# A two-layer Hyena and attention trunk on one core: attention listed ahead of Hyena, filter weights four weight blocks sooner, owed vector work capped after an opening, one skip addition fewer

## The chip, the cores and the metric

The kernel runs on one core of a Trainium2 chip. The metric is the device time of one execution in microseconds; runs are compared by their median.

## The reference

The input is one sequence of 256 positions with 1024 channels, in fp32. Two layers follow each other; each is a SwiGLU block (hidden width 2688), a mixer, and a second SwiGLU block, all with RMSNorm ahead and a residual behind. The mixer runs two branches on the same input and adds them through sigmoid gates:

```python
for l in range(DEPTH):
    x = x + 0.5 * swiglu(rms_norm(x, ffn1_norm[l]), ...)
    x = x + hybrid_mixer(rms_norm(x, mix_norm[l]), ...)
    x = x + 0.5 * swiglu(rms_norm(x, ffn2_norm[l]), ...)
# hybrid_mixer, branch A (Hyena): z, x1, x2 = short_conv3(h @ w_in[hyena])
kf = hyena_filters(...)          # sin(sin(z @ w1 + b1) @ w2 + b2) @ w3, decayed, normalised, rfft
for o, gate in enumerate((x1, x2)):
    z = gate * (long_conv(z, kf[:, o]) + hy_skip[o] * z)
# branch B (attention): q, k RMS-normed per head; 12 heads in 3 dilation groups; softmax over 193 strided keys
y = (sigmoid(gA) * (y_hy @ w_hy_proj) + sigmoid(gB) * (y_at @ w_at_proj)) @ w_out
```

## The kernel before

**Weights and slots.** Every product is fp32 accuracy made of three fp32r products (high times high, high times low, low times high). So each weight block of 128x1024 floats is loaded by the sync queue into one of four `raw` buffers, copied to its high half `whi` by the scalar engine (ACT, line 151), and subtracted to its low half `wlo` by the vector engine (DVE, line 58, the helper through which most vector work goes, so all of it carries that line). Seven `whi`/`wlo` pairs are in flight. TensorE (PE) uses one block in one *slot*, mostly 24 matmuls of 128x256 on line 89. I number the blocks of layer 0 as w0, w1, ... in the order of loading: w0 to w64 are the first SwiGLU block (`ffn(l, 1)`), w65 to w68 the first q/k block and w69 to w80 the Hyena columns of the mixer's projection, w81 to w94 the other q, k and v blocks, w95 to w110 the gates, w111 on the merges. Layer 1 repeats this.

**Order of the work.** The program is emitted under `manual_schedule`, so each engine runs its instructions in the order in which Python emits them. `slot()` first calls `tick(room)`, which advances generators ("side chains") that hold everything that isn't a weight block, then emits the matmuls. `retire` emits the `whi` and `wlo` of later blocks and the evacuation of the finished accumulator. `tick` goes through the list `side` in its order, and stops when `owed`, an estimate of the vector work emitted and not yet done, reaches `room`; `passed` takes 2.43 from it per slot. A chain that has just yielded True isn't taken up again until its own work is estimated done (`due`). `drain(ended, room)` advances the side chains without any slot between them until a condition holds.

**Side chains.** In `ffn(l, 1)` the chain is `filters(l)` (in layer 0 also `tables`): a product with `fc`, a sine (vector arithmetic on `sd`, then the scalar engine's Sin, line 578), a second such pair, `st`, then for each of two orders a slot `fw3_unit` with the third filter weight (where the constant `FW3` says: after the evacuation of row block m = 10 and m = 20, so at w22 and w43), the decay product `k`, squares `sq` whose sum is transposed on PE (`s<-ident,sq`), a power on GpSimd (POOL), `rb`, `nb`, and the Fourier products `s<-hl,dft` into `spec`. In the mixer the chains are `hyena()`, `attention()` and one `qknorm(blk)` per q/k block, which squares (`sq`, ACT), sums (`ss`, DVE), takes a power on POOL (`rs<-ss,mhalf`, line 877), multiplies (`qk<-qk,rs`, DVE) and transposes on PE (`x<-ident,qk`). `conv(pr)` evacuates a Hyena pair with taps on DVE (`c<-acc,cw,c`) and transposes it (`x<-ident,c`, line 750). One step of `attention()` is: transposes of the last scores (`x<-ident,at`), values (`x<-v,at`), and new scores (`x<-qkT,...`), which DVE biases and ACT exponentiates (line 934). `gate(m)` starts with a drain until `spec0` (m below 4) or `spec1` (m from 4 on) is in `ready`, which Hyena adds when it has read that part of `spec`; gate 4 begins at w103. After the last gate a drain runs all side chains to their ends, then the merges use Hyena's output `u` (high and low half) and attention's `yaT`.

**PSUM.** Accumulators `acc` rotate over 3 banks, `x` over 3, `s` over 2. In `ffn(l, 1)` row block m uses the same `acc` bank as m + 3, so the matmuls of m + 3 wait until the two vector instructions of m's evacuation (`t<-t,acc`) have read it.

Of the kernel before, what the change touches and what calls it, by code (L numbers as in the profile page):

```python
# [37 lines left out]
ROOM = (0.9, 2.2, 2.5, 1.5, 1.5)  # L38
OVER = 0.07
MARGIN = 0.2  # L40
UNIT = 2.43
DEFER = 4
LEAD = 1
FW3 = (10, 20)


@with_exitstack
def hybrid_trunk(ctx: ExitStack, tc: tile.TileContext, a: dict, out: bass.AP):
# [4 lines left out]
    owed = [0.0]  # L53
# [154 lines left out]
    def await_(g):  # L208
        due[g] = min(owed[0], 2 * UNIT)

    def tick(room):
        for g in list(urgent):
            if due.get(g, 0.0) <= MARGIN and step(g) == "end":
                urgent.remove(g)
        live = [g for g in side if due.get(g, 0.0) <= MARGIN]
        while live and owed[0] < room:
# [14 lines left out]
    def flush():  # L231
        if pend:
            done, evac = pend.pop()
            retire(evac, done)

    def slot(fn, w, done=1, evac=None, room=0.0):
        if pend and getattr(pend[0][1], "first", False):
            flush()
        if room:
            tick(room)  # L240
        flush()
        while ptr["lo"] <= w:
            pump_lo()
        fn(*pairs[w])
        passed(UNIT)
        pend.append((done, evac))
# [104 lines left out]
    def opening(acc, evac, n):  # L351

        us = [use() for _ in range(4)]
        per = n // P

        def part(i, j):
            g, k = divmod(i, per)
            return xstat({j: acc[j][g]}, k, n, (j,), g * n if acc[j][0] is acc[j][-1] else 0, j == 0 and i > 1)

        for i in range(4):  # L360
            while ptr["lo"] <= us[i]:
                pump(1)
            part(i, 0)(*pairs[us[i]])
            if i in FEAT1:
                features(1, i - FEAT1[0])()
            for _ in range(FILL[i]):
                pump(1)
        evac(0)
        for i in range(4):
            u = us[i]  # L370
            slot(part(u - us[0], 1), u, evac=(lambda: evac(1)) if i == 3 else None)


    def proj_out(nk, lhs, coef, gain, tags=("x", "acc", "acc", "acc")):
# [172 lines left out]
    def filters(l):  # L547
        def gen(fp):
# [47 lines left out]
            for o in range(2):  # L596
# [52 lines left out]
                for i in range(2):  # L649
                    for j in range(2):  # L650
                        t = sd[j, i]
                        TT(out=t, in0=t, in1=nb, op=ALU.mult)
                        if j == 0:
                            TT(out=t[0:1, :], in0=t[0:1, :], in1=sk[:, o, :], op=ALU.add)
                        yield False
                for i in range(2):
# [68 lines left out]
    def mixer(l, gain):  # L725
        with tc.tile_pool(name=nm("mix"), bufs=1, reuse_waits="tile") as mp:
# [265 lines left out]
            for blk in range(5):  # L992
                n = 512 if blk < 4 else 256
                acc = [bank("acc") for _ in range(2)]
                last = n // 128 - 1
                if blk == 0:
                    opening([[b] for b in acc], qkv_out(blk, n, acc), n)
                    gens = [hyena(), attention()]
                    side.extend(gens)
                    for pr in range(6):  # L1000
                        pb = bank("acc")
                        slot(wstat(pb, sls[0]), use(), room=ROOM[0])
                        slot(wstat(pb, sls[1]), use(), evac=conv(pr)(pb), room=ROOM[0])
                else:
                    out_j = qkv_out(blk, n, acc)

                    def both(f=out_j):
                        f(0)
                        f(1)

                    both.first = True
                    for i in range(last + 1):
                        slot(xstat(acc, i, n), use(), evac=both if i == last else None,
                             room=ROOM[1])
# [217 lines left out]
```

## Time and profile before

| | before |
|---|---|
| runs | 1118.97, 1120.11, 1120.43 us; median 1120.11 |
| profiled execution | 1119.33 us, span 1117.5 us |
| granted TensorE clock, mean | 0.999 |
| PE busy | 1102.4 us, 99% of the span |
| DVE, ACT, POOL busy | 840.2, 643.3, 64.4 us |
| chain that ended last | PE 82%, DVE 8%, DMA 5%, ACT 3% |

The profiled execution's time has 1.8 us outside the span. A share is of the span; a row of a timeline gives start, duration, engine, line, operation, output and inputs by the program's names, and in brackets the idle time just before it with what ended it.

### The profile page before, as it was taken

To read this page: it belongs to the slowest core of one execution; us is meant where nothing else is said; L and a number is where in the kernel's file an instruction comes from. 1 tells how busy PE (TensorE), PEld (TensorE's weight loads), DVE (VectorE), ACT (ScalarE), POOL (GpSimd) and SP (SyncE) were. 2 spreads that over 40 slices of the span, in tenths; PEclk is the share of its full clock that TensorE was granted. 3 is DMA by queue.
4 is the path that set the end of the run, shared out by engine and by line. 5 is a ranking of instruction groups with operands and counts; after the bars stand their busy time and mean duration, and the time that the engine had idled before them with its cause. 6 is when DMAs were issued, how large, how long until landed. Compare 5 with 4: busy or idle time off the path is not lost.

```text
span 1117.5 us, 19195 instructions
## 1 busy us (share of the span) xinstructions
PE 1102.4 (99%) x7591; PEld 1029.3 (92%) x7591; DVE 840.2 (75%) x1243; ACT 643.3 (58%) x983; POOL 64.4 (6%) x113
## 2 busy tenths in 40 slices
PE   9999999999999999999999999999999999999998
PEld 8999988998999999998899998889989998999997
DVE  6779896788865877777567789868888667777772
ACT  6566754665655556666456665547565554666651
POOL 5100000011200000000000000001012000000000
PEclk9999999999999999999999999999999999999999
DMA  8756666556433746667746665737465245666671
GB/s 302 234 168 210 201 212 184 170 171 189 150 115 108 234 140 201 195 193 235 252 147 201 192 209 174 244 110 240 156 185 156 86 125 205 200 192 193 189 256 64
DMA packets 58845, 206.35 MB, mean 185 GB/s; under 512 B 7058, under 2 KB 7718, under 8 KB 58756
## 3 DMA queue, kind: packets, MB, share of 16 engines
q1 hardware_dynamic: 57764, 203.10, 57.3%
q0 software_dynamic: 704, 1.97, 0.6%
q8 instruction: 59, 0.97, 0.4%
q14 instruction: 30, 0.25, 0.1%
q10 hardware_dynamic: 288, 0.07, 0.0%
HBM read 204.00 MB, written 1.11 MB: 184 GB/s over the span
## 4 chain that ended last, share of the span: by engine, by line
PE 82%; DVE 8%; DMA 5%; ACT 3%; issue 2%; POOL 0%; SPq 0%; ACTq 0%; DVEq 0%; POOLq 0%
PE acc L89 54%; PE x L89 13%; PE s L89 12%; DMA raw<-in_gu 4%; DVE wlo L58 3%; PE x L102 2%; DVE spec L58 1%; ACT whi L151 1%; DVE t L58 1%; DVE xn L58 1%; ACT sq L285 1%; DVE x L58 1%; DVE hT L58 1%; PE x L750 1%; PE s L102 0%
## 5 line engine op out<-in xcount | busy, mean ns | idle before, releaser
L58 DVE TENSOR_TENSOR wlo<-raw,whi 128x1024 fp32r<-128x1024 f32 (+1 forms) x380 | 457.6, 1210 | 54.8 <-ACT whi L151 54.5
L151 ACT ACTIVATE whi<-raw 128x1024 fp32r<-128x1024 f32 (+1 forms) x380 | 392.8, 1046 | 142.3 <-PE acc L89 52.6
L89 PE MATMUL acc<-hT,whi 128*128 128x256 f32 (+1 forms) x2416 | 463.5, 290 | 0.0
L89 PEld LDWEIGHTS acc<-hT,whi 128*128 128x128 f32 x2416 | 379.6, 192 | 8.2 <-issue 1.3
L89 PE MATMUL acc<-hT,wlo 128*128 128x256 f32 x1360 | 367.1, 275 | 0.0
L89 PEld LDWEIGHTS acc<-hT,wlo 128*128 128x128 f32 x1360 | 260.9, 192 | 1.9
L89 PE MATMUL acc<-whi,hid 128*128 128x512 f32 (+1 forms) x378 | 115.5, 357 | 0.0
L89 PE MATMUL acc<-whi,hT 128*128 128x256 f32 (+1 forms) x576 | 115.2, 328 | 0.0
L89 PE MATMUL x<-whi,hid 128*128 128x512 f32 x336 | 112.1, 380 | 0.0
L89 PE MATMUL s<-hT,whi 128*128 128x512 f32 x304 | 104.0, 383 | 0.0
L89 PEld LDWEIGHTS acc<-whi,hT 128*128 128x128 f32 x576 | 88.0, 191 | 8.6 <-ACT hT L317 1.1
L89 PEld LDWEIGHTS acc<-whi,hid 128*128 128x128 f32 x378 | 71.0, 189 | 8.6
L89 PE MATMUL s<-hT,wlo 128*128 128x256 f32 x304 | 76.7, 273 | 0.0
L89 PEld LDWEIGHTS x<-whi,hid 128*128 128x128 f32 x336 | 63.6, 189 | 7.9
L89 PE MATMUL acc<-wlo,hid 128*128 128x512 f32 (+1 forms) x189 | 66.4, 356 | 0.0
L89 PEld LDWEIGHTS s<-hT,whi 128*128 128x128 f32 x304 | 57.7, 190 | 6.9 <-DVE c L58 0.7
L89 PE MATMUL acc<-wlo,hT 128*128 128x256 f32 (+1 forms) x288 | 63.4, 324 | 0.4 <-DVE wlo L58 0.2
L89 PE MATMUL x<-wlo,hid 128*128 128x512 f32 x168 | 63.7, 379 | 0.0
L481 ACT ACTIVATE hid<-t 128x256 fp32r<-128x256 f32 x38 | 19.9, 523 | 70.1 <-DVE t L58 70.1
L89 PEld LDWEIGHTS s<-hT,wlo 128*128 128x128 f32 x304 | 58.1, 191 | 1.9
L58 DVE TENSOR_TENSOR hid<-t,hid 128x256 fp32r<-128x256 f32 x76 | 35.5, 466 | 22.4 <-ACT hid L481 22.4
L58 DVE SCALAR_TENSOR_TENSOR t<-t,acc 128x256 f32<-128x256 f32 x46 | 19.2, 417 | 43.0 <-ACT t L457 33.1
(189 smaller groups left out, 1297.4 us busy)
## 6 DMA issues: line engine op xcount, KB each, us to landing
raw<-in_gu SPq DMA_DIRECT2D x152, 512.0 KB, 4.3
raw<-in_dn SPq DMA_DIRECT2D x84, 512.0 KB, 4.4
raw<-in_win_q SPq DMA_DIRECT2D x32, 512.0 KB, 4.0
raw<-in_wg SPq DMA_DIRECT2D x32, 512.0 KB, 4.2
raw<-in_win_h SPq DMA_DIRECT2D x24, 512.0 KB, 4.5
raw<-in_gx SPq DMA_DIRECT2D x16, 512.0 KB, 5.0
raw<-in_wo SPq DMA_DIRECT2D x16, 512.0 KB, 4.1
raw<-in_wp SPq DMA_DIRECT2D x16, 384.0 KB, 3.0
```

What stands on the lines that cost most here:

```text
L58: return f(**kw)
L89: nc.tensor.matmul(o, l, r, start=start, stop=stop)
L102: nc.tensor.transpose(b[:, q * P:(q + 1) * P], ap, ident)
L151: act(out=pairs[v][0][:, :n], in_=raws[v][:, :n], func=AF.Copy)
L285: act(out=sq, in_=x[:, j, sl], func=AF.Square, scale=1.0 / 32.0, accum_out=nst[j][:, h:h + 1])
L481: act(out=hi, in_=tv, func=AF.Copy)
L750: nc.tensor.transpose(tb[j][:, (q0 + i) * P:(q0 + i + 1) * P], c[:, i, 1 + j:1 + S:2], ident)
```

## The change

Four edits. `opening()` (the first four blocks of a stage) ends by lowering `owed` to at most 2.0, so that side chains may go on sooner. `FW3` moves the first third-filter-weight slot from after m = 10 to after m = 8 (w22 to w18; the second stays at w43). The skip term is added only for i = 0, in place of i = 0 and 1: one vector addition of one row (1x512) fewer per order and layer, four in all; no reader sees another value, since the odd part's first row has a factor of zero. In the mixer `attention()` stands ahead of `hyena()` in the list of side chains.

```diff
--- before.py
+++ after.py
@@ -38,10 +38,11 @@
 ROOM = (0.9, 2.2, 2.5, 1.5, 1.5)
 OVER = 0.07
 MARGIN = 0.2
+OPEN = 2.0
 UNIT = 2.43
 DEFER = 4
 LEAD = 1
-FW3 = (10, 20)
+FW3 = (8, 20)
 
 
 @with_exitstack
@@ -369,6 +370,7 @@
         for i in range(4):
             u = us[i]
             slot(part(u - us[0], 1), u, evac=(lambda: evac(1)) if i == 3 else None)
+        owed[0] = min(owed[0], OPEN)
 
 
     def proj_out(nk, lhs, coef, gain, tags=("x", "acc", "acc", "acc")):
@@ -650,7 +652,7 @@
                     for j in range(2):
                         t = sd[j, i]
                         TT(out=t, in0=t, in1=nb, op=ALU.mult)
-                        if j == 0:
+                        if j == 0 and i == 0:
                             TT(out=t[0:1, :], in0=t[0:1, :], in1=sk[:, o, :], op=ALU.add)
                         yield False
                 for i in range(2):
@@ -995,7 +997,7 @@
                 last = n // 128 - 1
                 if blk == 0:
                     opening([[b] for b in acc], qkv_out(blk, n, acc), n)
-                    gens = [hyena(), attention()]
+                    gens = [attention(), hyena()]
                     side.extend(gens)
                     for pr in range(6):
                         pb = bank("acc")
```

No instruction is added. What moves is the order. Three places follow; the change's own lines are one higher (L59 for L58), and numbers behind a name tell buffers apart.

First place: DVE, first SwiGLU block of layer 0. `t` and `hid` belong to evacuations, `sd` to the sines. Before, from the evacuation of m = 3 (`acc_529`) to that of m = 4 (`acc_596`):

```order
L58 SCALAR_TENSOR_TENSOR t_607<-t_607,acc_529 128x256
L58 TENSOR_TENSOR t_607<-t_607,acc_529 128x256
L58 TENSOR_TENSOR wlo_567<-raw_473,whi_566 128x1024
L58 TENSOR_TENSOR hid_212<-t_607,hid_193 128x256
L58 TENSOR_TENSOR wlo_605<-raw_503,whi_604 128x1024
L58 SCALAR_TENSOR_TENSOR t_674<-t_674,acc_596 128x256
L58 TENSOR_TENSOR t_674<-t_674,acc_596 128x256
```

Now, from the block behind the evacuation of m = 3 to the evacuation of m = 4 (`acc_608`):

```order
L59 TENSOR_TENSOR wlo_579<-raw_473,whi_578 128x1024
L59 TENSOR_TENSOR hid_212<-t_619,hid_193 128x256
L59 TENSOR_TENSOR wlo_617<-raw_507,whi_616 128x1024
L59 TENSOR_SCALAR sd_238<-s_683,fc_231 128x256
L59 TENSOR_SCALAR sd_238<-sd_238 128x256 x2
L59 SCALAR_TENSOR_TENSOR sd_238<-sd_238 128x256 x3
L59 TENSOR_SCALAR sd_238<-sd_238 128x256
L59 SCALAR_TENSOR_TENSOR t_696<-t_696,acc_608 128x256
L59 TENSOR_TENSOR t_696<-t_696,acc_608 128x256
```

The whole second sine has moved in ahead of the evacuation of m = 4; the first sine stands with its first half ahead of the evacuation of m = 2 and with its second half ahead of that of m = 3. Before, both sines came behind m = 4.

Second place: DVE, start of the mixer. `ss` are the sums of the q/k norm, `rs` is POOL's power, `c` the Hyena taps. Before:

```order
L58 TENSOR_REDUCE ss_2662<-sq_2664 128x8
L58 TENSOR_TENSOR wlo_2667<-raw_2568,whi_2666 128x1024
L58 TENSOR_REDUCE ss_2662<-sq_2709 128x8
L58 TENSOR_SCALAR ss_2662<-ss_2662 128x16
L58 TENSOR_TENSOR wlo_2712<-raw_2601,whi_2711 128x1024
L58 SCALAR_TENSOR_TENSOR c_2426<-acc_2661,cw,c_2426 128x256 x4
L58 TENSOR_TENSOR u_2423<-x_2702,u_2422 128x512
L58 TENSOR_TENSOR u_2423<-x_2703,u_2422 128x512
L58 TENSOR_TENSOR wlo_2746<-raw_2635,whi_2745 128x1024
L58 TENSOR_TENSOR qk_2435<-qk_2435,rs_2663 128x512
```

Now:

```order
L59 SCALAR_TENSOR_TENSOR c_2424<-acc_2530,cw,c_2424 128x256 x4
L59 TENSOR_REDUCE ss_2562<-sq_2598 128x8
L59 TENSOR_SCALAR ss_2562<-ss_2562 128x16
L59 TENSOR_TENSOR wlo_2601<-raw_2522,whi_2600 128x1024
L59 TENSOR_TENSOR qk_2433<-qk_2433,rs_2563 128x512
L59 TENSOR_TENSOR wlo_2640<-raw_2536,whi_2639 128x1024
L59 SCALAR_TENSOR_TENSOR c_2425<-acc_2596,cw,c_2425 128x256 x4
L59 TENSOR_TENSOR qk_2433<-qk_2433,rs_2563 128x512
```

From the second sum to the product with `rs` there were seven rows between, now there are two; the first taps stand ahead of the second sum in both. On PE the transposes of `qk` came behind w78 and w80 and now come behind w73 and w74, those of the first `c` behind w73 and now behind w72.

Third place: PE, ahead of w103 (gate 4). `odd` is the room that holds the scores of head 2. Before, from the end of w102 to the first matmuls of w103:

```order
L102 MATMUL x_3749<-ident,at_3593 128x128 x4
L89 MATMUL x_3756<-v_2432,at_3593 128x64 x4
L89 MATMUL x_3763<-qkT_3269,qkT_2820 128x128 x2
L89 MATMUL x_3763<-qkT_3460,qkT_2820 128x128
L89 MATMUL x_3763<-qkT_3460,qkT_3269 128x128
L89 MATMUL acc_3782<-hT,whi_3513 128x256 x2
L89 MATMUL acc_3782<-hT,wlo_3514 128x256
```

Now:

```order
L103 MATMUL x_3748<-ident,at_3626 128x128 x4
L90 MATMUL x_3755<-v_2430,at_3626 128x64 x4
L90 MATMUL x_3762<-qkT_3274,qkT_2676 128x128 x2
L90 MATMUL x_3762<-qkT_3469,qkT_2676 128x128
L90 MATMUL x_3762<-qkT_3469,qkT_3274 128x128
L103 MATMUL x_3781<-ident,odd_3619 128x128 x4
L90 MATMUL x_3787<-v_2430,at_3626 128x64 x4
L90 MATMUL x_3794<-qkT_3274,odd_3618 128x128 x2
L90 MATMUL x_3794<-qkT_3469,odd_3618 128x128
L90 MATMUL x_3794<-qkT_3469,odd_3619 128x128
L90 MATMUL acc_3780<-hT,whi_3513 128x256 x2
```

Two steps of attention now follow each other in the drain with no slot between them, so `x<-ident,odd`, which reads the second row group's scores, comes right behind them; before, w103 lay between. Behind w110, before the merges, attention's last two values and its last transposes stood (`x<-ident,at`, `x<-v,at` twice, `x<-ident,ya`); now only Hyena's last transposes `s<-ident,tt` stand there, with the copy and subtraction into `u`, and attention has ended at w109.

## Rows read from the trace of the kernel before

**Rows 1.** The page: busy time, share of the span, instructions of each engine.

```profile
PE 1102.4 (99%) x7591; PEld 1029.3 (92%) x7591; DVE 840.2 (75%) x1243; ACT 643.3 (58%) x983; POOL 64.4 (6%) x113
```

**Rows 2.** Waits of PE, whole span: total us, times, longest.

```profile
PE s L89 <- DVE hl L58: 2.3, 2, 1.4
PE s L102 <- DVE sq L58: 1.5, 1, 1.5
PE x L89 <- DVE st L58: 1.2, 1, 1.2
```

**Rows 3.** Timeline, layer 0, start of the mixer: start, duration, engine, line.

```profile
219.80 1.66 DVE L58 SCALAR_TENSOR_TENSOR c<-acc,cw,c 128x256 f32<-128x256 f32 x4 [1.56 <-ACT c L770]
224.12 0.66 PE L750 MATMUL x<-ident,c 128*128 128x128 f32 x4
224.53 0.47 PE L89 MATMUL acc<-hT,whi 128*128 128x256 f32 x2
227.43 0.68 DVE L58 TENSOR_REDUCE ss<-sq 128x8 f32<-128x512 f32 x1
228.25 1.23 DVE L58 TENSOR_TENSOR wlo<-raw,whi 128x1024 fp32r<-128x1024 f32 x1
228.40 3.84 POOL L877 TENSOR_TENSOR rs<-ss,mhalf 128x16 f32<-128x16 f32 x1 [26.33 <-DVE ss L58]
```

**Rows 4.** The tile rs and its readers, whole span: ns min/median/max.

```profile
L58 DVE TENSOR_TENSOR qk<-qk,rs x12: 678/685/693, 233.8 to 848.5; 128x512 f32<-128x512 f32 x12
L877 POOL TENSOR_TENSOR rs<-ss,mhalf x6: 2898/3842/3850, 228.4 to 842.0; 128x16 f32<-128x16 f32 x6
```

**Rows 5.** Timeline, layer 0, an attention step: PE, DVE, ACT.

```profile
318.70 0.47 PE L89 MATMUL acc<-hT,whi 128*128 128x256 f32 x2
318.99 0.69 DVE L58 CUSTOM_DVE_ANT_0 odd<-x,bias 128x512 f32<-128x512 f32 x1 [0.66 <-PE x L89]
319.72 0.72 ACT L934 ACTIVATE odd<-odd,mx 128x512 f32<-128x512 f32 x1 [1.87 <-DVE mx L58]
320.35 0.19 ACT L934 ACTIVATION_READ_ACCUMULATOR odd<-odd,mx 128x1 f32 x1
321.46 0.60 PE L102 MATMUL x<-ident,odd 128*128 128x128 f32 x4
```

**Rows 6.** Timeline, layer 0, around the last gate slot: ACT, then PE.

```profile
350.27 0.60 ACT L858 ACTIVATE u<-s 128x512 fp32r<-128x512 f32 x1 [2.95 <-PE s L102]
355.81 0.82 ACT L1026 ACTIVATE spec<-acc,bg 128x256 f32<-128x256 f32 x2
354.98 0.60 PE L102 MATMUL x<-ident,at 128*128 128x128 f32 x4
357.17 1.10 PE L89 MATMUL x<-v,at 128*128 128x64 f32 x8 [0.76 <-ACT at L939]
358.66 0.33 PE L956 MATMUL x<-ident,ya 128*128 128x128 f32 x1 [0.27 <-DVE ya L58]
358.74 0.47 PE L89 MATMUL acc<-u,whi 128*128 128x256 f32 x2
```

**Rows 7.** Timeline, layer 0, first feed-forward block: DVE, PE, ACT.

```profile
45.91 0.42 DVE L58 SCALAR_TENSOR_TENSOR t<-t,acc 128x256 f32<-128x256 f32 x1 [3.19 <-ACT t L457]
56.73 0.70 PE L89 MATMUL s<-sd,fc 64*128 64x256 f32 x2 [0.58 <-ACT sd L578]
57.64 1.28 ACT L457 ACT_TABLE_LOAD   x1
58.93 0.38 ACT L457 ACTIVATE t<-acc 128x256 f32<-128x256 f32 x1
```

**Rows 8.** The tile sd, 40 to 70 us: ns min/median/max.

```profile
L58 DVE TENSOR_SCALAR sd<-sd x6: 293/293/318, 49.9 to 67.6; 128x256 f32<-128x256 f32 x6
L58 DVE SCALAR_TENSOR_TENSOR sd<-sd x6: 412/425/429, 53.5 to 67.2; 128x256 f32<-128x256 f32 x6
L578 ACT ACTIVATE sd<-sd x2: 416/416/417, 56.3 to 67.9; 128x256 f32<-128x256 f32 x2
```

## The prediction

> **What bounds the kernel now.** I read first the page's busy times: PE is busy 1102.4 of the 1117.5 us of the span [rows 1], so only some 15 us of its waiting can be won, and any new wait of PE lengthens the span by itself. No matmul is added or taken away, and the clock is near full, so the forecast is a sum over PE's waits: those that go, and those that come. Second I read the waits of PE. Those on the filter chain of the first SwiGLU blocks are: Fourier operands `hl` 2.3 in two places, `sq` 1.5, `st` 1.2 [rows 2], and the second filter product 0.58 [rows 7]. Third I read the timeline at the places where the order changes, with one question: how long after its last input does PE get what it asks for, and how much other PE work lies between. One slot of 24 matmuls is the measure of such cover: from 318.70 to 321.46 one takes 2.76 us with the switch of operand at its start [rows 5]; I count 2.7.
>
> **The profiled execution** took 1119.33 us, 0.78 below the median of the runs, 1120.11. The sum is made on 1119.33, and 0.78 is added at the end.
>
> **Mixer, start: +2.75 us per layer.** In the new order the q/k norm of the first block asks for POOL's power one slot before its product is needed. The four taps end at 219.80 + 1.66 = 221.46 [rows 3]; the second sum stands behind them and takes 0.68 [rows 3], to 222.1. POOL starts 0.29 after a sum ends (228.11 to 228.40 [rows 3]), so at 222.4. The power takes 2.90 to 3.85, median 3.84 [rows 4]. In the first instance a subtraction `wlo` starts at 228.25, 0.15 before it [rows 3], and the same `wlo` follows the sum now, so I take 3.84: ready at 226.25; the product, 0.69 [rows 4], ends at 226.95. PE ended w73 at 224.12; it now has the first transposes of `c` (0.41, from 224.12 to 224.53 [rows 3]) ahead of it, and wants `qk` at 224.6. It waits 2.35. The second product on DVE stands behind a `wlo` of 1.23 and four taps of 1.66 [rows 3]: 226.95 + 1.23 + 1.66 + 0.69 = 230.5, against 226.95 + 0.41 + 2.7 = 230.1 on PE, so 0.4 more. With the short power the first wait is 1.4 and the sum 1.8; with another 0.5 of delay on ACT, which now squares both halves ahead of the taps, it is 3.3. Behind the product, DVE's next `wlo` wait too; PE has pairs in stock for several slots, so that costs nothing here. Blocks 1 and 2 keep at least a slot and a Fourier product between power and transposes: 0.
>
> The Trainium skill says on the page "SBUF — State Buffer", section "Who interferes with whom", that a vector instruction with two SBUF inputs and a GpSimd instruction that reads SBUF exclude each other, and the second to issue blocks until the first is done. By that rule 228.25 + 1.23 − 228.40 = 1.08 of the 3.84 is blocking and the power is short wherever no `wlo` starts just ahead; with a short one in both layers the end sum below would be 1.9 lower.
>
> **Mixer, gate 4: +1.84 us per layer.** Two attention steps stand back to back in the drain. The same step in the trace shows the latency: PE has issued the scores by 318.70, DVE's biasing starts at 318.99, ACT's exponential at 319.72, and its accumulator is read by 320.35 + 0.19 = 320.54 [rows 5]. Before, the slot up to 321.46 covered it [rows 5]; now the transposes `x<-ident,odd` come at once and wait 320.54 − 318.70 = 1.84. This is pure latency of three engines; only what PE's own end is modelled wrong can shorten it, to 1.5 at least.
>
> **Mixer, end: +1.1 us per layer.** After w110, at 354.98, PE now has 0.4 of transposes and then the merge, whose second matmul reads the low half of `u`. ACT must first write the gate (355.81 + 0.82 = 356.63 [rows 6]), then `u`, 0.60 [rows 6], and DVE subtract, as the other 128x512 operations 0.69 [rows 4]: 357.9. So PE stands still about 357.9 − 354.98 − 0.5 = 2.4. Before, it waited 0.76 and 0.27 there [rows 6], and did its other work in the 3.76 us to 358.74 [rows 6]; that work isn't lost, it lies ahead of w110 now. The difference is 1.4 by the rows' idle times; these are counted from modelled ends, and by the issue times it is nearer 1.0. I take 1.1, and as bounds 0 (should `u` be first on ACT in fact) and 1.4.
>
> The mixer: 2.75 + 1.84 + 1.1 = 5.7 a layer, 11.4 in all; bounds 6.6 and 13.2.
>
> **First SwiGLU block: −2.6 us in all.** The filter chain starts seven blocks sooner. Gone: the wait for the first sine 0.58 [rows 7], since both sines now have slots between them and their readers; the wait for `st` 1.2 [rows 2], since `st` is made ahead of w18 by several slots; both waits for `hl`, 2.3 [rows 2], which came from two Fourier steps without a slot between, and now four blocks lie between them. That is 4.1. The wait for `sq` I leave: the sum and its transposes stand two slots apart as before, and the vector work between is the same.
>
> Against it stands a new wait for an `acc` bank. The evacuation of m = 4 ended at about 45.91 + 0.88 = 46.8 [rows 7]; the first matmul of m = 7, in the same bank, came two slots before 56.73 − 0.58 [rows 7], at 50.75. Of this margin of 3.95 us the two sines take more than all: each has four scalar operations of 0.29, three of 0.425 and the Sin of 0.42 [rows 8], 2.85, and each sends ACT to another table and back for the evacuation's Tanh, 1.28 [rows 7]. Twice 4.1 is 8.3; DVE sat idle 3.19 just before that evacuation [rows 7], which takes up some, so 5.1 later: 51.9. PE itself comes 0.6 later (the second small product, 0.7 with its modelled tail [rows 7], now lies ahead). The wait is 0.55 by this, and up to 2.5 if the idle time can't be used, as much of it was waiting for loads; I take 1.0, and in layer 1, where the trace shows no row that I can compare as closely, half of it. So −4.1 + 1.5 = −2.6. Bounds: −5.6, with no bank wait and `sq` gone too; +2.4, with 2.5 in both layers and `sq` new in layer 1.
>
> A rule that speaks against this step: the Trainium skill, page "ScalarE: Activation LUTs", section "What ACT_TABLE_LOAD costs", adds a drain of about 1.38 us to each load of 1.28. The row shows Tanh at 58.93, 0.01 after the load's end at 58.92 [rows 7], so no drain here. By that rule the two loads back to Tanh would add 2.8 to the bank wait of each layer, and the time would be 1134.5.
>
> **The rest: 0.** The skip additions saved lie on DVE, 75% busy [rows 1], four times some 0.7 in work that no wait of PE follows. The cap on `owed` acts through the order just counted. The earlier load of the filter weight moves one block in SP's queue by four places among equal blocks, and the skip row's small load some slots ahead with its chain; neither is waited for.
>
> **Sum:** 1119.33 + 11.4 − 2.6 = 1128.1; with 0.78, **1128.9 us**, 0.8% slower.
>
> **Rivals.** (1) *Faster.* The backlog of DVE is what feeds these waits, and starting side chains sooner takes it away everywhere: then POOL gets its inputs a slot sooner and the start of the mixer costs nothing, `u` is ready and the 1.03 at the end go too, and the filter chain gains its whole 5.6. Only gate 4 is left: 2 x (1.84 − 1.03) − 5.6 = −4.0, or 1116.1. It decides if the power starts by 220.0 instead of 222.4. For it: DVE has a quarter of its time free. Against: the taps ahead of the second sum began after 1.56 us of idling for ACT [rows 3], so DVE is not late there; PE's own pace sets the power's start. Chance 0.10. (2) *No change.* The mixer costs its lower bound 6.6 and the filter chain gains 5.6: 1121.1, or nothing if the end of the mixer is free as well. Chance 0.14. (3) *More slower.* DVE's order in the first SwiGLU block costs full bank waits, and `sq` too: 1120.1 + 11.4 + 2.4 = 1133.9. For it: until 56 us ACT and DVE idle for loads in that stretch, so the 3.19 may not be theirs to use. Against: the bank waits shorten the backlog behind them. Chance 0.09; a pause behind each table load, which [rows 7] rule out but for the place, would end near the same time, 0.01 more. (4) The change does nothing, since PE's order hides it: excluded in the main by gate 4, where no work lies between.
>
> **How the numbers follow.** The forecast has 0.66 and holds 1124 to 1132. A difference below 0.2% (2.2 us) can't be told from none. Faster than that is (1); the same is (2) and a small part of the forecast's low end; the rest is slower. The range from 1121 to 1133.5 leaves out (1), half of (2) at most, and the upper end of (3), 0.2 in all.
>
> **What would show it.** In the new profile: a wait of PE on `x<-ident,qk` near 224 of 1.4 to 2.4 us, ended by DVE's `qk`, with POOL's `rs` of 3.84 from about 222; a wait on `x<-ident,odd` of 1.8 in the drain before gate 4; a wait at `acc<-u,whi` or `u,wlo` after the last gate slot of about 2.4 against 1.03 there now; all three again in layer 1. In the first SwiGLU block no waits on `st`, on the first `sd` and on the second `hl`, and a wait of an `acc<-whi,hT` at w14 on DVE's `t`. The forecast is wrong if POOL's power starts a slot sooner, if `sq` and the bank waits are both gone, or if waits appear in blocks 1 and 2 of the mixer.

## The result, and the profile after

The changed kernel took 1133.05 us in the median of four runs (1131.30 to 1134.25), the kernel before beside it 1120.27 (1118.97 to 1120.71): a ratio of 1.0115 with an interval of 1.0097 to 1.0133, slower by 1.15%. The forecast was 1128.9 with a range of 1121.0 to 1133.5; the median lies 0.45 us under the upper end of that range, and two of the four executions lie above it. The profiled execution, the slowest of the four, took 1134.25 us with a span of 1132.5, against 1117.5 before: 15.0 us more.

The page's busy row comes first, for comparison with [rows 1]:

```profile
PE 1108.6 (98%) x7591; PEld 1034.7 (91%) x7591; DVE 839.1 (74%) x1239; ACT 643.6 (57%) x983; POOL 64.9 (6%) x113
```

PE has the same 7591 matmuls and is busy 6.2 us longer (1108.6 against 1102.4). Before anything else the reader should see that: no matmul was added, so some of them ran slower. The other 15.0 − 6.2 = 8.8 us are added time in which it stands still.

Next the waits of PE over the whole span (engine, line, what is waited for: total us, times, longest), to be held against [rows 2]; rows that are much the same before are left out:

```profile
PE x L103 <- DVE qk L59: 4.5, 2, 2.3
PE x L103 <- ACT odd L936: 3.3, 2, 1.6
PE acc L90 <- ACT u L860: 3.2, 2, 1.6
PE acc L90 <- DVE t L59: 2.2, 1, 2.2
PE s L103 <- DVE sq L59: 1.2, 1, 1.2
PE x L752 <- DVE c L59: 0.5, 1, 0.5
```

The waits on `st` and `hl` of [rows 2] are gone. In their place stand two on `qk`, two on `odd`, two on `u`, and one on `t`, the bank. Each of the first three comes once in each layer with the same length to within 0.1, so these are the mixer's order, not chance. The timeline shows where each comes from (start, duration, engine, line, operation). First the start of the mixer in layer 0, DVE, POOL and PE, which answers to [rows 3]:

```profile
219.78 1.66 DVE L59 SCALAR_TENSOR_TENSOR c<-acc,cw,c 128x256 f32<-128x256 f32 x4 [1.26 <-ACT c L772]
221.36 0.68 DVE L59 TENSOR_REDUCE ss<-sq 128x8 f32<-128x512 f32 x1
222.15 1.22 DVE L59 TENSOR_TENSOR wlo<-raw,whi 128x1024 fp32r<-128x1024 f32 x1
222.32 3.82 POOL L879 TENSOR_TENSOR rs<-ss,mhalf 128x16 f32<-128x16 f32 x1 [21.21 <-DVE ss L59]
226.18 0.69 DVE L59 TENSOR_TENSOR qk<-qk,rs 128x512 f32<-128x512 f32 x1 [2.80 <-POOL rs L879]
227.01 0.63 PE L103 MATMUL x<-ident,qk 128*128 128x128 f32 x4 [2.27 <-DVE qk L59]
```

The second sum ends at 222.04, the power starts at 222.32 with a `wlo` 0.17 ahead of it and takes 3.82, the product follows, and PE gets its transposes after 2.27 of idling. Layer 1 has the same rows, with the same 2.27 at 784.71. Next gate 4 in layer 0, PE, DVE, ACT and PE, against [rows 5]:

```profile
320.68 1.11 PE L90 MATMUL x<-qkT,qkT 128*128 128x128 f32 x8
321.82 0.69 DVE L59 CUSTOM_DVE_ANT_0 odd<-x,bias 128x512 f32<-128x512 f32 x1 [0.66 <-PE x L90]
322.56 0.72 ACT L936 ACTIVATE odd<-odd,mx 128x512 f32<-128x512 f32 x1 [1.86 <-DVE mx L59]
323.42 0.66 PE L103 MATMUL x<-ident,odd 128*128 128x128 f32 x4 [1.64 <-ACT odd L936]
```

The step is that of [rows 5], but between the scores, which PE has issued by 321.8, and the transposes that read them no matmul is left. Next the end of the mixer, ACT, DVE and PE, against [rows 6]:

```profile
362.47 0.82 ACT L1028 ACTIVATE spec<-acc,bg 128x256 f32<-128x256 f32 x2
363.18 0.60 ACT L860 ACTIVATE u<-s 128x512 fp32r<-128x512 f32 x1
363.81 0.69 DVE L59 TENSOR_TENSOR u<-s,u 128x512 fp32r<-128x512 f32 x1 [2.23 <-ACT u L860]
363.83 0.38 PE L90 MATMUL acc<-u,whi 128*128 128x256 f32 x1 [1.60 <-ACT u L860]
364.56 0.38 PE L90 MATMUL acc<-u,whi 128*128 128x256 f32 x1 [0.35 <-DVE u L59]
```

`u` is last on ACT, behind the gate's two Tanh, and then DVE takes the low half: 1.60 and 0.35 of idling where [rows 6] have 0.76 and 0.27. Next the bank wait in the first SwiGLU block, ACT, DVE and PE, against [rows 7]:

```profile
46.21 1.28 ACT L580 ACT_TABLE_LOAD   x1
50.13 0.42 ACT L580 ACTIVATE sd<-sd 128x256 f32<-128x256 f32 x1 [2.63 <-DVE sd L59]
51.51 1.28 ACT L459 ACT_TABLE_LOAD   x1
52.80 0.38 ACT L459 ACTIVATE t<-acc 128x256 f32<-128x256 f32 x1
53.67 0.42 DVE L59 TENSOR_TENSOR t<-t,acc 128x256 f32<-128x256 f32 x1
54.24 0.35 PE L90 MATMUL acc<-hT,whi 128*128 128x256 f32 x1 [2.25 <-DVE t L59]
```

ACT takes its instructions in the program's order. So between the table load for the second sine at 46.21 and the load back at 51.51 it doesn't come to the Tanh that is needed before the bank is free, and the 2.63 us that it idles there is for DVE's sine. DVE has read the bank at 53.67 + 0.42 = 54.09, and PE goes on at 54.24. Last the windows of PE around three of these waits (window, its length, then busy us and instructions of PE, PEld, DVE, ACT, POOL; then the granted clock, the DMA share and GB/s), each with the stretch behind it:

```profile
54.30:58.20 3.90, 3.90 (x21) 3.90 (x22) 3.80 (x6) 2.96 (x6) 0.00 (x0) 0.56 0.43 132
58.20:62.00 3.80, 3.80 (x36) 3.80 (x36) 3.74 (x6) 2.92 (x5) 0.00 (x0) 1.00 0.83 252
364.60:368.80 4.20, 4.20 (x23) 4.20 (x24) 0.77 (x1) 0.84 (x1) 0.00 (x0) 0.59 0.48 162
369.00:377.00 8.00, 8.00 (x74) 8.00 (x73) 7.14 (x10) 4.33 (x5) 0.00 (x0) 1.00 0.34 99
784.80:789.00 4.20, 4.20 (x24) 4.20 (x25) 4.20 (x8) 1.63 (x2) 0.00 (x0) 0.59 0.41 125
789.00:797.00 8.00, 8.00 (x73) 8.00 (x73) 5.44 (x10) 5.71 (x9) 0.00 (x0) 1.00 0.44 133
```

After the bank wait, after layer 0's wait on `u` and after layer 1's wait on `qk`, PE is busy without a gap and yet does 21 to 24 matmuls where it does 36 in 3.80 us, or 74 in 8.00, a moment later: the granted clock there is 0.56 to 0.59, which is mostly the lower of the two levels, 1.2 GHz. At the pace of the stretch behind, 21 matmuls would take 2.2 us, 23 take 2.5 and 24 take 2.6; so 1.7, 1.7 and 1.6 us are lost, 5.0 in all. The equal waits at 227.01, 323.42, 882.09 and 922.50 have no such stretch behind them.

### The profile page after: what moved, and what is told of

Its sections match the earlier page's. It is cut to its first block, busy times and chain, and to the rows that moved or that the text cites. A ratio compares the mean times of both kernels' runs of the same rounds, so it can differ in the third digit from the quotient of the medians.

```text
span 1132.5 us, 19202 instructions
## 1 busy us (share of the span) xinstructions
PE 1108.6 (98%) x7591; PEld 1034.7 (91%) x7591; DVE 839.1 (74%) x1239; ACT 643.6 (57%) x983; POOL 64.9 (6%) x113
## 3 DMA queue, kind: packets, MB, share of 16 engines
HBM read 204.00 MB, written 1.11 MB: 181 GB/s over the span
## 4 chain that ended last, share of the span: by engine, by line
PE 80%; DVE 7%; DMA 5%; ACT 4%; issue 3%; POOL 1%; SPq 0%; ACTq 0%; DVEq 0%; POOLq 0%
PE acc L90 52%; PE x L90 13%; PE s L90 12%; DMA raw<-in_gu 4%; DVE wlo L59 3%; PE x L103 2%; ACT whi L152 1%; DMA raw<-in_win_h 1%; DVE t L59 1%; DVE spec L59 1%; POOL rs L879 1%; DMA raw<-in_gx 0%; PE x L752 0%; DVE xn L59 0%; DVE sd L59 0%
## 5 line engine op out<-in xcount | busy, mean ns | idle before, releaser
L59 DVE TENSOR_TENSOR wlo<-raw,whi 128x1024 fp32r<-128x1024 f32 (+1 forms) x380 | 456.7, 1208 | 55.9 <-ACT whi L152 54.9
L90 PEld LDWEIGHTS acc<-hT,whi 128*128 128x128 f32 x2416 | 382.2, 193 | 10.9 <-issue 3.7
L59 DVE TENSOR_TENSOR hid<-t,hid 128x256 fp32r<-128x256 f32 x76 | 35.8, 471 | 22.6 <-ACT hid L483 22.6
L59 DVE SCALAR_TENSOR_TENSOR t<-t,acc 128x256 f32<-128x256 f32 x46 | 19.2, 418 | 41.8 <-ACT t L459 29.9
```

The source lines that it names most:

```text
L59: return f(**kw)
L90: nc.tensor.matmul(o, l, r, start=start, stop=stop)
```

## The experiments

**The theory** after the result: the time is the waits of PE that the order brings, place by place as the prediction has them, plus a stretch at the lower clock behind some of them. **The rivals**: DVE is late in general, so that waits turn up wherever one looks and a cure at one place moves them to the next; or the slower stretches have nothing to do with the waits. Besides, the four edits had not been told apart. The kernel before took 1117.7 to 1118.4 beside the experiments and 1120.27 beside the changed kernel, so kernels are compared by their ratio to it.

**1. The cap alone**

```diff
+        owed[0] = min(owed[0], OPEN)
```

> The kernel before with the cap on the owed vector work alone (the order of the side chains, the filter weight and the skip term as before). Theory A, the chain of waits read from the traces: the cap alone puts the first q/k norm of the mixer one slot early, so PE stands 2.2 to 2.4 us for x<-ident,qk in each layer and some 0.5 for x<-ident,c, followed in layer 1 by a stretch at the lower clock level of 1.6 to 1.9; it also starts the first SwiGLU's filter chain sooner, so the bank wait near 54 us is there, 2.2 and then 1.6 to 1.9 at the lower clock, and one wait for hl stays, since the filter weight still comes at the tenth block. No wait on x<-ident,odd of over 0.5, and the end of the mixer as before. In all +6 to +10 on the kernel before, 1126 to 1130. Rival, the prediction's own attribution: the order of the side chains sets the start of the mixer and the cap only the filter chain; then the qk wait is absent and the time is 1118 to 1122. Rival, the disorder is general and the cap's waits spread over all blocks: waits in blocks 1 and 2 of the mixer as well.

Measured: 1130.36, ratio 1.0116 (1.0092 to 1.0140), 13 us: as much as the whole change, and more than the 6 to 10 that were expected. Its waits of PE:

```profile
PE x L103 <- DVE qk L59: 4.5, 2, 2.3
PE x L103 <- ACT at L936: 3.3, 2, 1.6
PE s L90 <- DVE hl L59: 2.5, 2, 1.5
PE acc L90 <- DVE t L59: 1.1, 1, 1.1
```

The 2.27 on `qk` is there in both layers, the bank wait too, and `hl` stays. So the cap, not the order of the chains, makes the start of the mixer. One point was missed: at the end of the mixer two attention steps now stand back to back with Hyena still first, and PE waits 1.64 for `at` in each layer where [rows 6] have 0.76. The cap alone already brings the latency of [rows 5] out of its cover, at another place. In layer 1 this wait ends at 913.49 and is followed by the most costly slower stretch of that profile; here are its window and the next, read as those above:

```profile
913.60:920.40 6.80, 6.63 (x31) 6.34 (x32) 1.86 (x5) 0.98 (x2) 0.00 (x0) 0.50 0.05 20
920.40:927.00 6.60, 6.60 (x61) 6.60 (x60) 3.99 (x7) 3.68 (x4) 0.00 (x0) 1.00 0.28 83
```

At the pace of the second, the 31 matmuls of the first would take 3.35 us, so some 3.3 of its 6.63 busy us are lost.

**2. Attention first, alone**

```diff
-                    gens = [hyena(), attention()]
+                    gens = [attention(), hyena()]
```

> The kernel before with attention listed ahead of Hyena and nothing else. Theory A: two attention steps back to back ahead of gate 4 and u last on ACT at the end. PE waits 1.6 to 1.8 for x<-ident,odd and 1.6 to 2.0 for acc<-u in each layer, against 1.03 at the end before; nothing at x<-ident,qk; the first SwiGLU as before. 2 x (1.64 + 0.9) = +5.1, and up to 1.9 for each place that falls to the lower clock: 1125 to 1128. Rival, the waits of the mixer come from all parts together: each alone gives less, within 2 us of the kernel before.

Measured: 1124.37, ratio 1.0058 (1.0042 to 1.0075), 6.5 us. Its waits of PE:

```profile
PE x L102 <- ACT at L934: 3.3, 2, 1.6
PE acc L89 <- ACT u L858: 3.2, 2, 1.6
```

These are the changed kernel's 3.3 and 3.2 (the wait ahead of gate 4 bears the name `at` here), and there is none on `qk`. In waits the part costs alone what it costs in the whole.

**3. All but attention first**

```diff
-                    gens = [attention(), hyena()]
+                    gens = [hyena(), attention()]
```

> The changed kernel with Hyena listed first again: cap, filter weight and skip term stay. Theory A: the odd wait and the longer wait at u are gone, the qk wait of 2.2 stays in both layers, the first SwiGLU blocks win 1.3 in all as in the changed kernel. Of the +15 in span the +5 to +7 of the attention's order are taken back: 1125.5 to 1128. Rival, the start of the mixer follows from the order of the chains: then the qk wait goes too and the time is 1117 to 1120.

Measured: 1125.46, ratio 1.0070 (1.0051 to 1.0090), 7.8 us. The wait on `u` is gone; that on `odd` is replaced by the wait of 1.64 for `at` at the end, as in experiment 1. The `qk` wait stays, and its two instances show its cause (DVE, POOL, PE in layer 0, then POOL, DVE, PE in layer 1):

```profile
220.73 1.22 DVE L59 TENSOR_TENSOR wlo<-raw,whi 128x1024 fp32r<-128x1024 f32 x1
220.91 3.82 POOL L879 TENSOR_TENSOR rs<-ss,mhalf 128x16 f32<-128x16 f32 x1 [20.97 <-DVE ss L59]
225.59 0.63 PE L103 MATMUL x<-ident,qk 128*128 128x128 f32 x4 [2.27 <-DVE qk L59]
...
778.10 2.91 POOL L879 TENSOR_TENSOR rs<-ss,mhalf 128x16 f32<-128x16 f32 x1 [20.63 <-DVE ss L59]
778.28 1.22 DVE L59 TENSOR_TENSOR wlo<-raw,whi 128x1024 fp32r<-128x1024 f32 x1 [0.26 <-issue]
781.89 0.63 PE L103 MATMUL x<-ident,qk 128*128 128x128 f32 x4 [1.36 <-DVE qk L59]
```

Where a `wlo` has 1.04 left to run when the power starts, the power takes 3.82 and PE waits 2.27; where it starts 0.18 behind the power, the power takes 2.91 and PE waits 1.36. This is the pair of values that the prediction had for the long and the short power. The Trainium skill's rule, page "SBUF — State Buffer", section "Who interferes with whom" (such a vector instruction and a GpSimd instruction that reads SBUF exclude each other, and the second waits), agrees with the first instance, where the power came second. In the second instance the `wlo` came second, and by the rule it should have waited; it took its usual 1.22 from 0.18 behind the power's start. There the measurement decides: this case shows the rule in one direction only.

**4. The filter weight sooner, alone**

```diff
-FW3 = (10, 20)
+FW3 = (8, 20)
```

> The kernel before with the filter weight alone asked for sooner (FW3 at the eighth block instead of the tenth). Theory A: without the cap the chain makes st only one slot ahead of the product that now reads it, so PE waits longer for st than the 1.2 before, by about the two slots of 24 matmuls by which the reader moved, 2 x 2.7 in each layer: +5 to +11, 1125 to 1131. Rival: the edit moves a transfer and nothing that waits, within 2 us of the kernel before.

Measured: 1127.72, ratio 1.0090 (1.0072 to 1.0108), 10 us. The wait:

```profile
PE x L89 <- DVE st L58: 12.1, 2, 7.1
```

It is 7.1 in layer 0 and 4.9 in layer 1. By itself the edit asks for `st` before the chain can have made it.

**5. The changed kernel without the cap**

```diff
-        owed[0] = min(owed[0], OPEN)
```

> The changed kernel without the cap: attention first, filter weight sooner, skip term. Theory A: the start of the mixer is as in the kernel before (no wait on qk), the odd and u waits stay, 1.64 and 1.60 to 2.0 in each layer, and the filter weight without the cap costs its 5 to 7 on st in each layer. The sum of the two parts measured alone, +6.0 and +9.4 on the kernel before, is +15.4: 1131 to 1136, no faster than the changed kernel. Rival (the cap is the costly part and the kernel is better without it, as its +12 alone says): 1121 to 1126.

Measured: 1137.39, ratio 1.0159 (1.0136 to 1.0181), the slowest of all and above the 1131 to 1136 that were expected; its six executions have granted clocks of 0.988 to 0.995, and the profiled one, 1130.53, is the fastest of them. The wait of experiment 4 on `st` is back, 10.9 in two instances, and there is none on `qk`. The parts don't add: the cap costs 1.16% alone, yet taking it out of the whole costs another 0.44%, since it is what makes `st` in time for the sooner weight. Cap and sooner weight together (experiment 3, with the skip term) cost 0.70%, less than the cap alone; against the 0.90% of the sooner weight alone the intervals overlap.

**6. The skip term twice again**

```diff
-                        if j == 0 and i == 0:
+                        if j == 0:
```

> The changed kernel with the skip term added in both halves again (four additions of one row more on DVE). Theory A: no wait of PE follows them: within 1.5 us of the changed kernel. Rival (DVE's owed work is the bound everywhere): +2 or more.

Measured: 1132.17, ratio 1.0127 (1.0107 to 1.0147): it can't be told from the changed kernel. The waits on `qk`, `odd` and `u` are 4.5, 3.3 and 3.2 as before.

**7. One slot more ahead of the first product**

```diff
+                if blk == 0:
+                    yield True
```

> The changed kernel with one slot more between POOL's power and the product in the first block's q/k norm, so that PE has a slot of 24 matmuls ahead of the transposes it stood for. Theory A (the power's 3.84 on POOL started too late for the slot that reads it): the wait of 2.27 on x<-ident,qk goes in both layers, nothing takes its place, and the slower stretch behind one of them goes with it: -4.5 to -6.5 against the changed kernel, 1126.5 to 1128.5. Rival (DVE is late in any case, so the product or what it feeds is late one slot further on): a wait on x<-ident,qk or x<-ident,c of 1 us or more stays, and the gain is under 2 us.

Measured: 1127.68, ratio 1.0090 (1.0076 to 1.0104), by the ratios 0.25% less than the changed kernel, with intervals that just overlap. The 2.27 is gone at the first block, and a new wait of 1.66 stands at the second, in both layers; here is layer 0, POOL and PE:

```profile
274.81 3.28 POOL L879 TENSOR_TENSOR rs<-ss,mhalf 128x16 f32<-128x16 f32 x1 [50.55 <-DVE ss L59]
278.97 0.52 PE L103 MATMUL x<-ident,qk 128*128 128x128 f32 x3 [1.66 <-DVE qk L59]
```

So the rival is right in part: the chain of the second block moved against Hyena's by one slot, and lost the Fourier product that lay between its power and its transposes. A stall moved along the same chain; by the two profiles the net gain is some 0.6 a layer and the slower stretch behind the first.

**8. Attention held while PE drains ahead of gate 4**

```diff
+                    while held[0]:
+                        yield True
```

> The changed kernel with attention held back while PE drains the last slots ahead of gate 4, so that its two last steps don't stand back to back there. Theory A (the 1.64 is the latency of scores, biasing and exponential with no work of PE between): the wait on x<-ident,odd goes in both layers, -3.3; what is held back then lies between the last gate and the merge, and the wait there grows or falls in pieces by up to 2 a layer: -3 to +1 on the changed kernel, and the qk wait of 2.27 unchanged. Rival (the wait comes from a late bias or late DVE, not from the order): a wait on odd of over 1 stays.

Measured: 1125.07, ratio 1.0063 (1.0051 to 1.0076), 0.5% less than the changed kernel, more than was expected. Its waits:

```profile
PE s L103 <- DVE sq L59: 4.2, 2, 2.7
PE x L103 <- DVE qk L59: 3.6, 2, 2.3
PE acc L90 <- ACT u L861: 1.4, 2, 0.7
PE s L103 <- DVE tt L59: 1.1, 2, 0.6
```

None on `odd` is left, and the end of the mixer got better, not worse: on `u` 0.7 where it was 1.6, with 0.6 on `tt` ahead of it. So the 1.64 was the order's alone. The `qk` wait is untouched: 2.27, and 1.36 in layer 1, where the power was the short one. The longest waits are now those on `sq` in the first SwiGLU blocks, 2.71 in layer 0 and 1.46 in layer 1. The edit doesn't reach layer 0's block, so this is how far that wait moves between executions.

**9. PE fed during the waits**

```diff
+    def feed(b, n):
+        for _ in range(n):
+            mm(b[:, :S], hT[:, 0, 0, 0, :], hT[:, 0, :, 0, :].rearrange("p j c -> p c j"), True, True)
...
+                    if blk == 0 and j == 0:
+                        feed(b, 18)
...
```

> The changed kernel with matmuls whose results nothing reads put into four of its waits: 18 ahead of the first q/k transposes and 13 ahead of gate 4's transposes and of the first merge, in both layers, and 18 at the bank wait of layer 0; each matmul takes 0.112, so they fill 1.5 to 2.0 us of waits that are there anyway. Theory A (the stretches at the lower clock come from PE standing still): the waits themselves shrink to under 0.8, the granted clock is full behind them, and the time falls by the slower stretches alone, three of some 1.7 in the profiled execution: -3 to -6, 1127 to 1130. Rival (the slower stretches have another cause, such as a time in the execution): they stay, and the time is the same or up to 2 us longer, 1132 to 1135.

Measured: 1128.51, ratio 1.0105 (1.0085 to 1.0125). Two of its windows, at the places that were slow:

```profile
54.00:58.00 4.00, 4.00 (x39) 4.00 (x38) 3.83 (x6) 3.06 (x6) 0.00 (x0) 1.00 0.71 244
364.00:368.00 4.00, 4.00 (x38) 4.00 (x38) 3.20 (x5) 2.27 (x4) 0.00 (x0) 1.00 0.16 66
```

The profile has no slower stretch until its last 0.2 us, and three of five executions a granted clock of 1.000 and two of 0.998; of the changed kernel's four, none is above 0.997. The work that was fed is 106 matmuls, 11.9 us, and the time did not rise. But the ratio's interval overlaps with the changed kernel's, so the gain itself isn't settled by this run.

**10. The long waits fed**

Experiment 4 has longer waits, each with a slower stretch behind it, so the same is tried there (the edit against experiment 4, with `feed` as above; the line that counts the layers is left out):

```diff
+                    if o == 0 and not (j or d):
+                        feed(bs[0, 0], 58 if fstate["n"] == 1 else 40)
```

> The kernel before with the filter weight alone asked for sooner, and matmuls whose results nothing reads put into the two waits on st that this brought: 58 in layer 0 and 40 in layer 1, of 0.112 each, so 6.5 and 4.5 of waits of 7.15 and 4.93. Theory A (a long wait costs its length and then a stretch at the lower clock): the waits shrink to under 1 each, PE's other work starts at the same time, no slower stretch follows, every execution shows a granted clock of 0.997 or more, and the time falls by what the slower stretches took, 2.8 and 1.6 in that kernel's profile: a ratio of 1.003 to 1.006 where it was 1.009. Rival (the lower clock does not come from PE standing still): the clock stays at 0.989 to 0.994 and the ratio at 1.009 or above.

Measured: 1124.18, ratio 1.0051 (1.0038 to 1.0065), against 1.0090 (1.0072 to 1.0108): some 4 us less, with 98 matmuls more. The stretch behind the wait in layer 0, first without:

```profile
71.50:76.60 5.10, 5.10 (x18) 4.38 (x17) 3.11 (x7) 4.03 (x6) 0.00 (x0) 0.50 0.21 84
```

and then with the feeding:

```profile
71.00:76.00 5.00, 5.00 (x40) 4.81 (x40) 3.02 (x6) 4.03 (x7) 0.00 (x0) 1.00 0.24 90
```

The clock is at 0.50 in the one and full in the other, and the executions show 0.998 to 1.000 where they showed 0.989 to 0.994. The profile has no slower stretch behind either wait; the one that it has is at the end of layer 0's mixer, where nothing was fed. The lower clock comes from PE standing still. What a wait costs is its length and, behind some, the slower stretch.

**11. The cap in the SwiGLU blocks only**

```diff
-        owed[0] = min(owed[0], OPEN)
+        if cap:
+            owed[0] = min(owed[0], OPEN)
...
-            opening(acc, first, 256)
+            opening(acc, first, 256, True)
...
-                    gens = [attention(), hyena()]
+                    gens = [hyena(), attention()]
```

> Cap, filter weight and skip term, with the cap only at the openings of the SwiGLU blocks, and Hyena listed first: what the changed kernel has ahead of and behind the mixer, and the mixer of the kernel before. Theory A: no wait on qk, none on odd; the end of the mixer as before (0.76 and 0.27); in the first SwiGLU blocks the bank wait of 1.4 to 2.3 stays and the waits on st and the second hl are gone: -1 to -4 on the kernel before. Rival (the sooner filter chain only moves DVE's lateness into the mixer): 0 to +4.

Measured: 1116.52, ratio 0.9988 (0.9973 to 1.0002), which can't be told from the kernel before: the mixer is as it was, and the sooner filter chain gains little, with a bank wait of 1.0 and waits on `sq` of 1.8 and 1.0.

**12. The same, with the sines spaced**

```diff
-                yield False
+                yield True
...
-                        yield False
+                        yield True
```

> As the last one, with the vector steps of both sines set a slot apart each, so that the evacuation that frees the bank comes ahead of the second sine. Theory A (the bank wait is the two sines' time on DVE ahead of that evacuation): the bank wait near 53 us falls under 0.5 and the slower stretch with it: another -1.5 to -3, -3 to -6 on the kernel before. Rival (the bank is late by ACT's table loads or the weights): the bank wait stays over 1 us, and the time is that of the last kernel; or the second sine comes late itself and PE waits over 1 us on the second sd.

Measured: 1114.06, ratio 0.9965 (0.9954 to 0.9975). The bank wait is gone, and no wait on the second `sd` has come. Of the waits that are left, the longest is 1.70 on `hT`, which ends at 9.43 us, ahead of all that the edits move; the mixer's `at` has 1.5 in two instances, as before, and `sq` 1.3. This kernel is 0.35% faster than the one before, and by the ratios 1.5% faster than the changed one. Whether spacing the sines alone would do as much was not run.

## Why the prediction was right, and where it was off

**The sum of waits held.** The span grew by 15.0 us. Without the three slower stretches, 5.0, it is 10.0; the prediction's terms made 8.8. By the stages below, the 10.0 is 11.8 in the mixers, −3.0 in the first SwiGLU blocks, and some 1.1 in the start and the second SwiGLU blocks, which the prediction put at 0: these blocks take 168.28 and 173.11 where they took 167.90 and 172.48. That the two stages with terms make exactly 8.8 is in part luck, as the single terms show. It is luck in part, too, that the median fell into the range: it lies outside the 1124 to 1132 that was given 0.66.

**Mixer.** Start: 2.75 was forecast, of it 2.35 ahead of the first product and 0.4 ahead of the second. The first is 2.27, and the power started at 222.32 where 222.4 was worked out; the second is some 0.15 by the start times in layer 0 and nothing in layer 1, but the first transposes of `c` wait 0.55 in layer 0, which no term had. Gate 4: 1.84 forecast, 1.64 measured; the prediction counted from 318.70, 0.29 ahead of the biasing, while PE's wait begins at the modelled end of the scores, 320.68 + 1.11 = 321.79, 0.03 ahead of it. End: 2.4 forecast where 1.95 came, 0.92 above [rows 6] where 1.1 was taken. None of these terms is off by more than 0.5. The first transposes of the normalised input mark the stages: the mixer of layer 0 runs from 195.89 to 402.32, 206.43 against 198.13 before, and that of layer 1 takes 204.97 against 198.13. That is 15.1 more, and 11.8 without the stretches at 364.60 and 784.80, where 11.4 was forecast. The waits read here make some 10.4 of it; the rest stands in no wait that was read. (Two slips that change nothing: the upper bound of the mixer's sum, 13.2, is 13.1 by its own terms, 3.3 + 1.84 + 1.4 in each layer; and in the order before, six rows lie between the second sum and the product, not seven.)

**First SwiGLU block.** The waits on `st`, on the first `sd` and on both `hl` went, as counted. The bank wait came out at 2.25 in layer 0, where 1.0 was taken from between 0.55 and 2.5, and at none in layer 1, where 0.5 was. The evacuation ended at 54.09, 2.2 after the 51.9 that was worked out, so ACT and DVE could use only about 1 us of the idle 3.19. (With none of it used, the prediction's own rows give 46.8 + 8.3 = 55.1 and a wait of 3.75, not 2.5.) But 2.25 is one execution's number: up to this place ACT and DVE run the same instructions in the same order in experiments 3, 6, 7, 8 and 11, and these profiles have 1.36, 2.04, 0.62, 0.92 and 0.99. So the 1.0 isn't refuted, and what moves this wait from one execution to the next stays open. The `sq` wait was left unchanged, and is 1.24 in layer 1 instead of 1.5 in layer 0; in these runs it goes from under 0.3 to 2.7, so it is no firm term either. The two stages are 1.05 and 0.26 shorter, 1.3 together, and 3.0 without the slower stretch, where 2.6 was forecast. The rule of a drain on top of each table load, from the Trainium skill, page "ScalarE: Activation LUTs", section "What ACT_TABLE_LOAD costs", found no support here either: the load at 51.51 ends at 52.79 and Tanh starts at 52.80.

**The step that failed** is in the first paragraph: "the clock is near full, so the forecast is a sum over PE's waits". The trace of before gave no reason to doubt it, since its waits of 1.0 to 1.5 us have no slower stretch behind them. (The 51 executions of that kernel beside the experiments show 0.995 to 1.000, so it has such stretches at times too.) The new waits are longer, and three of them in the profiled execution cost 1.6 to 1.7 us on top; the 4.15 us between the forecast and the median are of that size. An estimate from the granted clocks of the four executions, (1 − clock) times the span, says that the lower clock took 5.7, 3.4, 3.4 and 6.8 us, to within 0.6; without it they are at 1127.2 to 1128.7, close to the forecast. Experiments 9 and 10 show the cause: with PE fed the lower clock is gone behind the fed waits, and in experiment 10 the time falls with it. The Trainium skill, page "TensorE: Matmul & The Clock Gate", section "Part 1: The HAM clock gate", says that the array's clock is halved by default and that activity releases it; the runs agree, as the clock fell behind waits and rose again while PE worked. What the sum left out is that a new wait carries a chance of a price beyond its length.

**The third rival's number**, 1133.9, is nearer to the result than the forecast's, but not its mechanism: there is one bank wait, not two, and `sq` is no worse.

**One statement was loose**: that the cap "acts through the order just counted". Experiment 1 shows that the cap alone makes the start of the mixer, the largest term; the order of the chains makes only gate 4 and the end. The forecast for the whole was not touched by that, but a reader who had kept the cap and dropped the order would have been misled.

**Left open** is why of two equal waits one is followed by a slower stretch and the other not, and how much the changed kernel's own median would fall without them: experiment 9's interval is too wide to say.

## What to carry to other kernels

When a bound engine waits, price the wait at its place in the order: latency of the chain since its last input, minus the work of that engine in between. When waits on TensorE grow from about 1 us to 2, add to the sum a chance of a further 1.7 us each, the price in most cases here, for the lower clock behind them. Undo the parts of a change one by one before judging any: here the part that cost most alone is needed by another; kept to one stage, with Hyena first and the sines spaced, it is part of a faster kernel.

## What the runs showed of the hardware

In the profiled executions of all these kernels but the one before, after the first 20 us, PE idled 11 times for 2.0 to 2.8 us and a stretch of reduced clock followed 7 of them; of 28 waits of 1.6 to 1.8 it followed 6, each time within 2 us of the wait's end; of the 16 waits of 1.0 to 1.5, none. With the four between 4.8 and 7.2 it came every time, during the wait or right behind it. In three profiles it came at the end of the mixer behind waits of under 0.8 that stand close together. Such a stretch took 1.6 to 1.8 us more than the same matmuls at full clock in most cases, 2.1 and 2.8 behind two of the longest waits, and 3.3 in three cases at the end of the mixer, in experiments 1 and 3. The executions of one kernel differ by it: experiment 3 took 1123.76 with a granted clock of 1.000, and 1130.81 with 0.992.

The power on POOL took from 2.90 us to 3.85 for the same 128x16 elements, by what DVE was running at its start: 2.90 or 2.91 where nothing was under way, 3.28 where a DVE operation of 0.69 with two inputs had begun 0.17 ahead, 3.81 to 3.85 where a `wlo` of 1.22 had begun 0.14 to 0.17 ahead. Once, in the changed kernel at 277.35, it took 5.02 with the same row ahead of it as those of 3.28; why stays open, and PE didn't wait for it. For a chain that waits for the power the long value is the one to plan with.
